# Loads of the sums in another order, stores of the down-projection on GpSimd's queue, and one pause more in the last norms, in a one-core decoder layer

## The chip, the cores and the metric

One Trainium2 chip; the kernel uses one of its cores. The metric is the device time of one execution in microseconds, as the median of several runs. The engines are called PE (TensorE's matmuls, with PEld for its weight loads), DVE (VectorE), ACT (ScalarE), POOL (GpSimd) and SP (the queue that issues nearly all DMAs).

## What is computed

A decoder layer over x of 1 x 2048 x 1024 in float32: two token mixers side by side, an output projection, a feed-forward part with a short causal convolution, and a final norm.

```python
def _conv_ffn(h, w_up, conv_w, conv_b, w_down):
    u = h @ w_up                                   # 1024 -> 2 x 2816
    u = causal_depthwise_conv(u, conv_w) + conv_b  # width 3
    gate, val = jnp.split(u, 2, axis=-1)
    return (jax.nn.silu(gate) * val) @ w_down      # 2816 -> 1024

def reference(x, ...):
    proj = _rmsnorm(x, norm1_w) @ w_in
    o_hg = _hgrn2_mixer(...)     # gated linear recurrence
    o_rw = _rwkv7_mixer(...)     # data-dependent decay, delta rule
    x = x + jnp.concatenate([o_hg, o_rw], axis=-1) @ w_out
    x = x + _conv_ffn(_rmsnorm(x, norm2_w), w_up, conv_w, conv_b, w_down)
    return _rmsnorm(x, final_norm_w)
```

## The kernel before

**Stages.** The 2048 tokens are four blocks of 512 (`b` = 0 to 3). Phase 1 (to some 1380 us) computes the mixers; the output projection of the last block follows (to some 1444 us), then the up-projection with convolution and gate (to some 2325 us), then the down-projection and the final norm (to the end). Every float32 matrix product is made of three matmuls (lines 262 to 264, `mm3`): an operand is split into a high part by ScalarE (line 246) and a low part by VectorE (line 247), and high x high, high x low and low x high are added up.

**The up-projection** (`run`, line 1345 on) has 44 iterations n: two halves of the tokens (two blocks each) x 22 groups of 128 columns. Each multiplies 2 x 2 blocks by a scheme of seven products instead of eight. A product (`prod`) is 4 x 3 = 12 matmuls of 128 x 512, so an iteration is 84 matmuls; the accumulators are called ua, ub and ud. Of each iteration's last two products and of its convolution (`late`: line 1424 on, the `y` of lines 1441 and 1442) the program speaks after the next iteration's first product. The result of the gate goes to DRAM as `gd` (line 1449).

**Side work.** After each product `aside(n)` (line 1305) takes one item off a list; an empty item is a pause of one product. Items are taken from n = 1 on, and none at n = 20 to 22. The list holds, in this order:
- `norm_last`, four times (blocks 2 and 3, two halves each): load two tiles `xt2` of x, pause, scale one tile, scale the other (line 1253), pause, then eight pairs of transposes on PE (`tp`, line 256), each with an eviction and a store to `h2d`. 13 items each.
- `four`, 15 times: load four tiles, pause, two items of VectorE work and four stores, pause: 5 items. They make the second half's transformed activations `Ts` and the transformed down weights `Tw`.
- `sums(g, kk)`, from n = 23 on: of the gate's results of one token half g the four tiles a11, a12, a21, a22 (first index the block, second the half of the 2816 columns) are loaded from `gd`, combined by four VectorE operations (line 1293), and each result is stored to `Sg` right after its operation (line 1294). 7 items: the loads, two pauses, four operations. Group 0 has all its kk = 0 to 10 there (n = 23 to 33), group 1 has kk = 0 to 6, one for each of n = 36 to 42.

All these tiles come from the ring `br`, six buffers of 128 x 512 that are given out in the order of release (`raw_`, line 1121). So a list of loads also says which tile gets a free buffer first. A tile scheduler sets the order on each engine. SP works through its queue in order: a DMA that waits holds all behind it.

**The down-projection** (line 1453 on) takes steps 5 to 142. A step needs one tile of gate results or sums and one of weights (`draw`, line 1462, six buffers per name), split into `da` and `db`, for 12 matmuls; `load(s_ + 4)` and `take(s_ + 2)` run ahead. The last four `sums` of group 1 are made here by `g_sums` (four `sraw` loads, four operations at lines 196 to 199, four stores at line 201), at four steps six apart. When the last product of a tile of tokens is done, `finish` scales the finished rows (line 1491) and stores them, 512 KB each (line 1493): eight stores for the first half of the tokens, in mid-stage, eight for the second, at the end. The residual tiles `xt3` (line 1476) have twelve buffers for sixteen tiles, so the last four loads go into buffers that the first half's output was stored from.

Of the kernel before, what the change touches and what calls it, by code (L numbers as in the profile page):

```python
# [18 lines left out]
P = 128  # L19
T = 2048  # L20
D = 1024
KD = D // P
# [39 lines left out]
def tile_layer(ctx, tc, consts, x, norm1_w, w_in, hg_lb_logits, hg_norm_w, rw_shift_mu, rw_w0, rw_w2,  # L62
               rw_a0, rw_a2, rw_g2, rw_k_k, rw_k_a, rw_r_k, rw_ln_w, rw_ln_b, w_out, norm2_w, w_up,
               conv_w, conv_b, w_down, final_norm_w, out, pairs=(0, 1, 2, 3), heads=(0, 1, 2, 3),
               stages=("1", "2"), dbg=None):
    nc = tc.nc
    V, S, TE = nc.vector, nc.scalar, nc.tensor
    dma = nc.sync.dma_start

    cp = ctx.enter_context(tc.tile_pool(name="cp", bufs=1, reuse_waits="tile"))  # L70
    dp = ctx.enter_context(tc.tile_pool(name="dp", bufs=1, space=DRAM))
# [22 lines left out]
    def pst(name):  # L94
        return pools["ps"].tile([P, 512], F32, tag="mm", name=name, bufs=8)
# [13 lines left out]
    def act(out_, in_, func, **kw):  # L109

        want = tables.get(func)
        if want is not None and want != tab["now"]:
            pre = S.preload_act_table_set(want)
            for u_ in tab["uses"]:
                tc.add_manual_dep(pre.ins, u_.ins.name, NOSYNC, reason="table order")
            tab.update(now=want, pre=pre, uses=[])
        i_ = S.activation(out_, in_, func, **kw)  # L117
        if want is not None:
            tc.add_manual_dep(i_.ins, tab["pre"].ins.name, NOSYNC, reason="table order")
            tab["uses"].append(i_)  # L120
        return i_

    def rstd(pool, xt, name, sqt="nsq", sqb=1):

        sq = pool.tile([P, D], BF16, tag=sqt, name="nsq", bufs=sqb)
        st = pool.tile([P, 2], F32, tag="nst", name=name, bufs=8)
        act(sq, xt, AF.Square, accum_out=st[:, 0:1])
        act(st[:, 1:2], st[:, 0:1], AF.Ln, bias=eps6, scale=1.0 / D)
        act(st[:, 1:2], st[:, 1:2], AF.Exp, scale=-0.5)
        return st[:, 1:2]  # L130
# [48 lines left out]
    gd_ = [dp.tile([FF, BLK], F32, name=f"gd{b}") for b in range(NBLK)]  # L179
# [3 lines left out]
    Sg = [[dp.tile([KH * P, BLK], F32, name=f"Sg{g}{i}") for i in range(4)] for g in range(2)]  # L183
    Tw = [dp.tile([KH * P, BLK], F32, name=f"Tw{i}") for i in range(4)]

    def krows(t_, q, kk):

        return t_[(q * KH + kk) * P:(q * KH + kk + 1) * P, :]
# [4 lines left out]
    def g_sums(tile_, g, kk):  # L193

        a11, a12, a21, a22 = (tile_(krows(gd_[2 * g + u], q, kk)) for u in range(2) for q in range(2))
        V.tensor_add(a22, a21, a22)
        V.tensor_sub(a21, a11, a21)
        V.tensor_sub(a11, a22, a11)
        V.tensor_sub(a12, a12, a11)
        for i, t_ in enumerate((a22, a11, a21, a12)):  # L200
            dma(krows(Sg[g][i], 0, kk), t_)


    DP = (("a", (0, 0), (0, 0)), ("b", (0, 1), (1, 0)), ("a", 1, 1), ("b", 0, 0), ("a", 2, 2), ("a", (1, 1), 3),
# [904 lines left out]
    with ExitStack() as c2:  # L1109
# [11 lines left out]
        def raw_(src):  # L1121
            t_ = hr.tile([P, BLK], F32, tag="br", name="br", bufs=6)
            if src is not None:
                loader[0](t_, src)
            return t_
# [20 lines left out]
        with tc.tile_pool(name="op", bufs=1, reuse_waits="tile") as op_:  # L1146
# [52 lines left out]
            for dh in range(2):  # L1199
                accs = [pst("wacc") for _ in range(4)]  # L1200
                for n, k in enumerate((0, 1, 4, 5, 2, 3, 6, 7)):
# [3 lines left out]
                    if n == 5:  # L1205
                        for i in range(4):
                            t0 = b * BLK + i * P
# [11 lines left out]
                    if dh == 1 and 2 <= n:  # L1219
                        for j in range(2):  # L1220
                            q = 2 * (n - 2) + j
# [9 lines left out]
        with tc.tile_pool(name="up", bufs=1, reuse_waits="tile") as up:  # L1231
# [7 lines left out]
            def aside_of(fs):  # L1239

                side.extend((first_at[0], f) for f in fs)

            def norm_last(b, i2):

                xt = []

                def load():
                    for q in range(2):
                        xt.append(up.tile([P, D], F32, tag="xt2", name="xt2", bufs=2))
                        dma(xt[q], x1d[b][(i2 * 2 + q) * P:(i2 * 2 + q + 1) * P, :])  # L1250

                def scale(q):
                    V.tensor_scalar_mul(xt[q], xt[q], rstd(hr, xt[q], "nst", "br", 6))

                def evict(k, tp, w):
                    t_ = hr.tile([P, 256], F32, tag="br", name="h2", bufs=6)
                    act(t_, tp, AF.Copy, scale=w)
                    dma(h2d[b][k * P:(k + 1) * P, i2 * 256:i2 * 256 + 256], t_)

                g = transposed(xt, "n2", lambda: pst("tp"), evict)  # L1260
                aside_of([load, None, lambda: scale(0), lambda: scale(1), None] + [lambda: next(g)] * KD)

            def four(srcs, make, dsts):

# [13 lines left out]
            QB = [(q, b) for q in range(2) for b in range(2)]  # L1278
# [8 lines left out]
            def sums(g, kk):  # L1287

                ts = []
                ops = ((3, V.tensor_add, 2, 3), (2, V.tensor_sub, 0, 2), (0, V.tensor_sub, 3, 0), (1, V.tensor_sub, 1, 0))  # L1290

                def op(d, f, a, b, i):
                    f(ts[d], ts[a], ts[b])
                    dma(krows(Sg[g][i], 0, kk), ts[d])

                aside_of([lambda: ts.extend(raw_(krows(gd_[2 * g + u], q, kk)) for u, q in QB), None, None]
                         + [lambda o=o, i=i: op(*o, i) for i, o in zip((0, 2, 1, 3), ops)])

            for g in range(2):
# [155 lines left out]
    with tc.tile_pool(name="dn", bufs=1, reuse_waits="tile") as dn:  # L1455
        ops, xts, pend, m2 = {}, {}, [], {}
# [32 lines left out]
        def finish(g, u, i):  # L1489
            t_ = xts.pop((g, u, i))  # L1490
            V.scalar_tensor_tensor(t_, t_, rstd(dn, t_, "fst"), fw, ALU.mult, ALU.mult)
            t0 = (2 * g + u) * BLK + i * P
            dma(out[0, t0:t0 + P, :], t_)

        def evict(g, p, accs, i):

# [20 lines left out]
        for s_ in range(DS, N):  # L1517
            g, p, kk = steps[s_]
# [60 lines left out]
```

## Time and profile before

| | |
|---|---|
| median of 3 runs | 2740.66 us (2735.97 to 2741.07) |
| the profiled execution | 2734.05 us; its span 2732.2 us |
| granted TensorE clock, mean | 0.991 |
| busy: PE, DVE, ACT, POOL | 96%, 69%, 49%, 13% of the span |
| DMA | 517.88 MB, mean 190 GB/s |

The profile is of one execution, which was 6.6 us shorter than the median of the runs; 1.85 us of it lie around the span. In a row of waits an engine's idle time is put down to what came last before it went on: `PE ua L262 <- ACT m L117: 5.6, 6, 1.5` says that PE, about to run line 262 into `ua`, waited for the ScalarE instruction that wrote `m`, for 5.6 us in total, 6 times, 1.5 us at the longest. A timeline row has start, duration, engine, line, operation and, in brackets, the idle time before it.

### The profile page before, as it was taken

How to read it: one execution, taken by the hardware profiler on the slowest of the kernel's cores; microseconds unless marked ns; L12 is line 12 of the kernel's file. 1: busy time of each engine (PE TensorE's matmuls, PEld its weight loads, DVE VectorE, ACT ScalarE, POOL GpSimd, SP SyncE). 2: the span in 40 equal slices, each digit the busy share in tenths (PEclk: the TensorE clock that was granted, in tenths of full speed). 3: DMA queues.
4: the chain of work that ended last, by engine and by line, in shares of the span. 5: the costliest groups of instructions: out<-in, count | busy, mean ns of one | idle time of the engine just before them, and what ended most of it. 6: DMA issues, size and time to landing. Idle time of an engine off the chain costs nothing.

```text
span 2732.2 us, 47983 instructions
## 1 busy us (share of the span) xinstructions
PE 2631.2 (96%) x18059; PEld 2097.0 (77%) x18059; DVE 1896.6 (69%) x3665; ACT 1348.1 (49%) x2168; POOL 367.5 (13%) x660
## 2 busy tenths in 40 slices
PE   7989999989999999999899999999999999999998
PEld 5767777767777767777677788887888877788887
DVE  4856656566456654756668789988888888677556
ACT  4546443444544335334456765456555445445444
POOL 6433222212321113222100000000000000000000
PEclk9999999999999999999999999999999999999999
DMA  8655544354663546854576358746655454898665
GB/s 299 198 162 165 171 138 134 115 147 156 215 199 105 138 140 212 280 143 132 165 245 192 119 193 268 234 151 222 222 187 194 132 191 131 287 320 289 213 193 185
DMA packets 365438, 517.88 MB, mean 190 GB/s; under 512 B 97439, under 2 KB 194069, under 8 KB 365205
## 3 DMA queue, kind: packets, MB, share of 16 engines
q1 hardware_dynamic: 313265, 345.39, 39.4%
q0 software_dynamic: 51872, 169.41, 19.2%
q8 instruction: 142, 2.33, 0.4%
q14 instruction: 91, 0.75, 0.1%
q10 hardware_dynamic: 68, 0.02, 0.0%
HBM read 376.27 MB, written 138.41 MB: 188 GB/s over the span
## 4 chain that ended last, share of the span: by engine, by line
PE 68%; DVE 11%; DMA 9%; issue 6%; ACT 4%; SPq 1%; POOL 1%; DVEq 0%; ACTq 0%; POOLq 0%
PE pj L262 8%; PE pj L263 7%; PE pj L264 7%; PE ua L262 4%; PE ua L264 4%; PE ua L263 4%; PE da L262 3%; PE da L263 3%; PE da L264 3%; PE ud L264 2%; PE ud L262 2%; PE ud L263 2%; PE db L263 2%; PE db L262 2%; PE db L264 2%
## 5 line engine op out<-in xcount | busy, mean ns | idle before, releaser
L262 PE MATMUL pj<-hh,wh 128*128 128x512 f32 x960 | 402.7, 420 | 2.2 <-ACT rkv L117 1.1
L263 PE MATMUL pj<-hl,wh 128*128 128x512 f32 x960 | 378.4, 394 | 0.0
L264 PE MATMUL pj<-hh,wl 128*128 128x512 f32 x960 | 378.4, 394 | 0.0
L262 PE MATMUL ua<-Bh,uwh 128*128 128x512 f32 x704 | 276.7, 393 | 7.2 <-ACT m L117 5.6
L264 PE MATMUL ua<-Bh,uwl 128*128 128x512 f32 x704 | 274.4, 390 | 0.0
L263 PE MATMUL ua<-Bl,uwh 128*128 128x512 f32 x704 | 274.2, 389 | 0.0
L262 PEld LDWEIGHTS pj<-hh,wh 128*128 128x128 f32 x960 | 181.0, 189 | 55.6 <-issue 12.2
L264 PEld LDWEIGHTS pj<-hh,wl 128*128 128x128 f32 x960 | 181.0, 189 | 40.1 <-DMA wl<-Win170l 0.6
L263 PEld LDWEIGHTS pj<-hl,wh 128*128 128x128 f32 x960 | 181.4, 189 | 39.1 <-issue 6.2
L246 ACT CAST uwh<-uraw 128x512 fp32r<-128x512 f32 x220 | 134.5, 617 | 139.3 <-PE ua L263 61.8
L247 DVE TENSOR_TENSOR dal<-draw,dah 128x512 fp32r<-128x512 f32 x138 | 95.3, 690 | 112.5 <-ACT dah L246 112.3
L247 DVE TENSOR_TENSOR uwl<-uraw,uwh 128x512 fp32r<-128x512 f32 x220 | 147.1, 686 | 36.3 <-ACT uwh L246 36.3
L246 ACT CAST dah<-draw 128x512 fp32r<-128x512 f32 x138 | 85.8, 622 | 166.2 <-PE da L263 74.5
L262 PEld LDWEIGHTS ua<-Bh,uwh 128*128 128x128 f32 x704 | 132.2, 188 | 37.4 <-ACT m L117 8.9
L264 PEld LDWEIGHTS ua<-Bh,uwl 128*128 128x128 f32 x704 | 132.1, 188 | 28.2 <-DVE uwl L247 0.4
L263 PEld LDWEIGHTS ua<-Bl,uwh 128*128 128x128 f32 x704 | 132.3, 188 | 26.7
L262 PE MATMUL ud<-Bh,uwh 128*128 128x512 f32 x352 | 137.7, 391 | 0.0
L264 PE MATMUL ud<-Bh,uwl 128*128 128x512 f32 x352 | 137.1, 389 | 0.0
L263 PE MATMUL ud<-Bl,uwh 128*128 128x512 f32 x352 | 137.0, 389 | 0.0
L263 PE MATMUL da<-dbl,dah 128*128 128x512 f32 x332 | 129.5, 390 | 0.2 <-DVE dbl L247 0.2
L264 PE MATMUL da<-dbh,dal 128*128 128x512 f32 x332 | 129.2, 389 | 0.0
L1449 POOL DMA_DIRECT2D gd<-y x2 | 1.1, 554 | 952.0 <-DVE y L1447 952.0
(567 smaller groups left out, 6189.3 us busy)
## 6 DMA issues: line engine op xcount, KB each, us to landing
uraw<-in_w_up_dram SPq DMA_DIRECT2D x176, 256.0 KB, 3.3
woraw<-in_w_out_dram POOLq DMA_DIRECT2D x96, 256.0 KB, 3.5
br<-gd SPq DMA_DIRECT2D x88, 256.0 KB, 4.4
draw<-Sg SPq DMA_DIRECT2D x88, 256.0 KB, 3.3
draw<-Tw SPq DMA_DIRECT2D x88, 256.0 KB, 3.4
gd<-y SPq DMA_DIRECT2D x86, 256.0 KB, 2.9
Sg<-br SPq DMA_DIRECT2D x72, 256.0 KB, 2.3
xt<-x1d SPq DMA_DIRECT2D x32, 512.0 KB, 6.5
```

Of the source, the lines that this page charges most:

```text
L246: S.copy(hi, src)
L247: V.tensor_sub(lo, src, hi.bitcast(F32))
L262: TE.matmul(acc, lh, rh, start=first, stop=False, skip_group_check=skip)
L263: TE.matmul(acc, lh, rl, start=False, stop=False, skip_group_check=skip)
L264: TE.matmul(acc, ll, rh, start=False, stop=last, skip_group_check=skip)
L1449: (dma if end is None else nc.gpsimd.dma_start)(gd_[2 * h + b][fb * P:(fb + 1) * P, :], ys[0][:, b * BLK:(b + 1) * BLK])
```

## The change

```diff
-    dma = nc.sync.dma_start
+    dma, store = nc.sync.dma_start, nc.gpsimd.dma_start
...
         for i, t_ in enumerate((a22, a11, a21, a12)):
-            dma(krows(Sg[g][i], 0, kk), t_)
+            store(krows(Sg[g][i], 0, kk), t_)
...
-                aside_of([load, None, lambda: scale(0), lambda: scale(1), None] + [lambda: next(g)] * KD)
+                aside_of([load, None, lambda: scale(0), lambda: scale(1), None, None] + [lambda: next(g)] * KD)
...
-                ops = ((3, V.tensor_add, 2, 3), (2, V.tensor_sub, 0, 2), (0, V.tensor_sub, 3, 0), (1, V.tensor_sub, 1, 0))
+                ops = ((1, V.tensor_add, 0, 1), (0, V.tensor_sub, 2, 0), (2, V.tensor_sub, 1, 2), (3, V.tensor_sub, 3, 2))
...
-                aside_of([lambda: ts.extend(raw_(krows(gd_[2 * g + u], q, kk)) for u, q in QB), None, None]
+                aside_of([lambda: ts.extend(raw_(krows(gd_[2 * g + u], q, kk)) for u, q in QB[2:] + QB[:2]), None, None]
...
-            dma(out[0, t0:t0 + P, :], t_)
+            (dma if g else store)(out[0, t0:t0 + P, :], t_)
```

Four parts. The norms get one pause more before their transposes, so each has 14 items, two whole iterations. The sums load a21, a22, a11, a12 instead of a11, a12, a21, a22; `ops` is renumbered for it, and the four operations are the same ones in the same order (a22 = a21 + a22, a21 = a11 - a21, a11 = a22 - a11, a12 = a12 - a11). The stores of `g_sums` (16 of 256 KB) and the first half's output stores (8 of 512 KB) are issued by GpSimd instead of SP.

**The sums of group 1, SP.** One iteration between n = 36 and 42; `gd_156` holds a11 and a12, `gd_157` a21 and a22, and `Sg_162` to `Sg_165` are where the four results go. Before:

```order
L1141 DMA uraw<-in_w_up_dram 128x4x128
L1124 DMA br<-gd_156 128x512
L1124 DMA br<-gd_157 128x512 x2
L1294 DMA Sg_165<-br 128x512
L1124 DMA br<-gd_156 128x512
L1294 DMA Sg_162<-br 128x512
L1294 DMA Sg_164<-br 128x512
L1141 DMA uraw<-in_w_up_dram 128x4x128
L1294 DMA Sg_163<-br 128x512
```

Now:

```order
L1141 DMA uraw<-in_w_up_dram 128x4x128
L1124 DMA br<-gd_157 128x512
L1124 DMA br<-gd_156 128x512 x2
L1124 DMA br<-gd_157 128x512
L1294 DMA Sg_162<-br 128x512
L1294 DMA Sg_164<-br 128x512
L1294 DMA Sg_163<-br 128x512
L1294 DMA Sg_165<-br 128x512
L1141 DMA uraw<-in_w_up_dram 128x4x128 x3
```

Before, a group of loads was a12, a21 and a22, and the next kk's a11 came behind a store of the kk before; now it is a22, a11 and a12, with the next kk's a21 right behind, and the four stores stand together.

**The same iteration, VectorE.** Line 1293 is an operation of the sums, `uwl` the low part of an up weight, `y1` the convolution's first accumulation. In the numbered names of the rows before, br_22574 is a11, 22576 a12, 22578 a21 and 22580 a22:

```order
L247 TENSOR_TENSOR uwl_22435<-s1_22412,uwh_22434 128x512
L1293 TENSOR_TENSOR br_22580<-br_22578,br_22580 128x512
L1293 TENSOR_TENSOR br_22578<-br_22574,br_22578 128x512
L247 TENSOR_TENSOR uwl_22452<-uraw_22306,uwh_22451 128x512
L1293 TENSOR_TENSOR br_22574<-br_22580,br_22574 128x512
L1441 SCALAR_TENSOR_TENSOR y1_22375<-cv_22213,cvt_14639,y1_22375 128x1024
```

In the rows now, br_22572 is a21, 22574 a22, 22576 a11 and 22578 a12:

```order
L247 TENSOR_TENSOR uwl_22433<-s1_22410,uwh_22432 128x512
L1293 TENSOR_TENSOR br_22574<-br_22572,br_22574 128x512
L1293 TENSOR_TENSOR br_22572<-br_22576,br_22572 128x512
L1293 TENSOR_TENSOR br_22576<-br_22574,br_22576 128x512
L1293 TENSOR_TENSOR br_22578<-br_22578,br_22576 128x512
L247 TENSOR_TENSOR uwl_22450<-uraw_22304,uwh_22449 128x512
L1441 SCALAR_TENSOR_TENSOR y1_22373<-cv_22211,cvt_14639,y1_22373 128x1024
```

The third operation moves ahead of the weight split, and the fourth, which before ran in the next iteration (ahead of that iteration's `uwl` of `s1`), joins the block.

**The first `g_sums` in the down-projection, SP.** `draw` are a step's two loads, `sraw` the loads of the sums, `xt` a residual tile. The piece of the difference, with - for rows of before and + for rows of now (the tile `xt` only has another number):

```order
-L1477 DMA xt_23623<-x1d_147 128x1024
-L201 DMA Sg_162<-sraw 128x512
-L201 DMA Sg_163<-sraw 128x512
-L201 DMA Sg_164<-sraw 128x512
-L201 DMA Sg_165<-sraw 128x512
+L1477 DMA xt_23621<-x1d_147 128x1024
 L1462 DMA draw<-Sg_159 128x512
 L1462 DMA draw<-Tw_167 128x512
```

The four stores stood between two steps' loads; now the next step's loads follow the residual tile directly. The same four rows stand on GpSimd's queue, where nothing else is left by then.

**The third norm, PE.** `tp` are the transposes of one 128 x 128 piece, `ua` and `ud` accumulators. The first transposes before:

```order
L262 MATMUL ud<-Bh_14661,uwh 128x512
L263 MATMUL ud<-Bl_14662,uwh 128x512
L264 MATMUL ud<-Bh_14661,uwl 128x512
L256 MATMUL tp<-ident,xt_16037 128x128
L262 MATMUL ua<-Bh_14664,uwh 128x512
L263 MATMUL ua<-Bl_14665,uwh 128x512
```

And now:

```order
L262 MATMUL ua<-Bh_14658,uwh 128x512
L263 MATMUL ua<-Bl_14663,uwh 128x512
L264 MATMUL ua<-Bh_14658,uwl 128x512
L256 MATMUL tp<-ident,xt_16072 128x128
L256 MATMUL tp<-ident,xt_16074 128x128
L262 MATMUL ud<-Bh_15084,uwh 128x512
```

They stood between an iteration's sixth and seventh product and now stand behind the second product of the next round, three products on: one for its own pause and one for each of the two norms ahead of it. Its loads move two products on, so from load to transposes it is one product more.

## The prediction

> **What bounds the kernel now.** I read the busy table first, then the stages as windows, then what TensorE waited for.
>
> ```profile
> PE 2631.2 (96%) x18059; PEld 2097.0 (77%) x18059; DVE 1896.6 (69%) x3665; ACT 1348.1 (49%) x2168; POOL 367.5 (13%) x660
> ```
>
> ```profile
> 1600.00:1800.00 200.00, 199.94 (x887) 165.15 (x886) 188.97 (x299) 104.12 (x152) 0.00 (x0) 1.00 0.75 246
> 1988.41:2140.73 152.32, 152.32 (x673) 126.13 (x672) 134.37 (x197) 77.53 (x112) 0.00 (x0) 1.00 0.53 171
> 2140.73:2283.15 142.42, 138.13 (x604) 112.72 (x603) 119.04 (x175) 67.66 (x100) 0.00 (x0) 1.00 0.56 183
> ```
>
> The window rows give length, then busy time of PE, PEld, DVE, ACT and POOL, clock, DMA share and GB/s. I set their bounds on the VectorE addition of line 1408, which runs once in every iteration n of the up-projection. The second is eight iterations with the sums of group 0: 152.32 / 8 = 19.04 us each, and PE is busy for all of it. The third is seven iterations (from n = 35's addition to n = 42's) with the sums of group 1: 142.42 / 7 = 20.35 us each, PE idle for 4.29 us, the clock full in both. So TensorE sets the pace nearly everywhere, and the change can win only where TensorE waits. Those places from the up-projection on:
>
> ```profile
> PE ua L262 <- ACT m L117: 5.6, 6, 1.5
> PE fa L263 <- DVE uwl L247: 2.6, 2, 1.6
> PE da L262 <- ACT dbh L246: 2.4, 1, 2.4
> PE ua L262 <- ACT uwh L246: 1.5, 1, 1.5
> PE tp L256 <- DVE xt L1253: 1.0, 1, 1.0
> ```
>
> Columns: total, times, longest. The six waits of 5.6 us are all in the sums of group 1 (the window 2140.73 to 2302 alone gives the same row); the 2.4 stands at 2384 in the down-projection; the 1.0 is the third norm's. These three, 9.0 us together, are what the edits touch. The `fa` waits (at n = 22) and the `ua` wait for `uwh` (at the first iteration) stay: no edit moves anything there. In phase 1, before 1380 us, nothing changes.
>
> **Part 1, the pause (line 1261).** Each of four norms gets one empty slot more between its scaling and its transposes. A slot is one product, 12 matmuls. This is the chain around the third norm's first transposes (start, duration):
>
> ```profile
> 1555.57 0.76 DVE xt L1253
> 1556.34 0.04 issue
> 1556.38 0.55 PE tp L256 x3
> 1556.93 0.23 PE ua L262
> ```
>
> The scaling (`xt`) ends at 1556.33 and the transposes start at 1556.38, after 0.96 us of idle TensorE (the row of 1.0 above). One product is 12 x 0.23 = 2.8 us. Put behind another product, the transposes would be due 1.8 us after the scaling is done: the wait goes, **-0.96**. Nothing else is late there, for the matmuls that move ahead have their operands (the same iteration has no other wait). The other three norms did not wait before and get more room. The bounds are 0 (if VectorE comes to the scaling as much later) and -0.96; I take -0.96, as with 14 slots, two whole iterations, every norm stands in the phase of the first one, which did not wait.
>
> The queue of side work grows by four slots: 4 x 14 + 15 x 5 = 131 slots, and n = 1 to 19 have 19 x 7 = 133. So the transformed tiles (`four`) run four products later and still end in n = 19. I cost that at nothing: their loads and stores are SP's and TensorE is busy 199.94 of 200 us there. The cover is VectorE's remaining 11 us in 200, about 1 us per iteration; if the new phase were worse, the nearest row is a wait like the norm's, 1.0 us, up to three times: 0 to +3, I take 0.
>
> **Part 2, the order of the sums' loads (lines 1290 and 1296).** In the sums of group 1 VectorE, not TensorE, sets the 20.35 us:
>
> ```profile
> DVE br L1293 <- DMA br<-gd: 22.0, 7, 3.7
> ```
>
> ```profile
> 2170.01 0.69 DVE L247 TENSOR_TENSOR uwl<-s,uwh 128x512 fp32r<-128x512 f32 x1
> 2174.07 1.42 DVE L1293 TENSOR_TENSOR br<-br 128x512 f32<-128x512 f32 x2 [3.38 <-DMA br<-gd]
> 2175.41 0.68 DVE L247 TENSOR_TENSOR uwl<-uraw,uwh 128x512 fp32r<-128x512 f32 x1
> 2176.01 0.68 DVE L1293 TENSOR_TENSOR br<-br 128x512 f32<-128x512 f32 x1
> 2176.61 1.28 DVE L1441 SCALAR_TENSOR_TENSOR y<-cv,cvt,y 128x1024 f32<-128x1024 f32 x1
> ```
>
> ```profile
> 2168.05 1.41 SPq L1124 DMA_DIRECT2D br<-gd  x3
> 2169.98 0.32 SPq L1294 DMA_DIRECT2D Sg<-br  x1
> 2170.35 0.42 SPq L1124 DMA_DIRECT2D br<-gd  x1
> ```
>
> VectorE works 119.04 / 7 = 17.0 us per iteration and waits 3.4 for `br`; 17.0 + 3.4 = 20.4. The first of a tile's four operations (2174.07) adds a21 to a22. SP issues a12, a21 and a22 from 2168.05 in 1.41 us, 0.47 each: a22 is the **third**, asked for at 2169.0, there at 2174.0; behind a store follows the next k's a11 (2170.35). In the new program a21 is loaded an iteration ahead and a22 is the first of the group, then a11 and a12; the four operations stand in one block.
>
> With the same issue times a22 is asked for at 2168.05 and a11 and a12 at 2168.5 and 2169.0. The first load of a group shares the engines with fewer. Its ends: the 5.0 us of the third (landing at 2173.0), and the 3.3 of SP's weight loads of this size (the `uraw` row below; landing at 2171.4). The operations take 0.69 each, a12 is needed by the fourth alone and lands at 2174.0 as the third load did. With the early end three operations run before 2174.0, the fourth ends at 2174.7, `uwl` runs, and `y` starts at 2175.3 instead of 2176.61: 1.3 saved. With the late end four operations end at 2175.8 and `y` starts at 2176.4: 0.2 saved. I take **0.8** per iteration, about the middle. VectorE's cycle becomes 20.35 - 0.8 = 19.55 us (19.05 to 20.15) against TensorE's 19.04.
>
> Before, VectorE fell behind by 7 x (20.35 - 19.04) = 9.2 us, and TensorE lost 5.6: so 3.6 us were covered by products whose operands were ready. Now it falls behind by 7 x 0.51 = 3.6 us, just that cover; I leave 0.3 for an uneven iteration: **-5.3**. At 20.15 the lag would be 7.8, of which 4.2 are lost, so the bounds are -1.4 and -5.6.
>
> In the sums of group 0 no wait reached TensorE (152.32 of 152.32 busy). The new program asks for all tiles of the next k there an iteration ahead, so I cost it at nothing; what hides a wait there is VectorE's idle time, (152.32 - 134.37) / 8 = 2.2 us per iteration. What it costs if this cover goes is the third rival.
>
> **Part 3, the stores of the late sums (line 201).** SP around the first of four, its wait, and TensorE behind it:
>
> ```profile
> 2374.57 0.32 SPq L1477 DMA_DIRECT2D xt<-x1d  x1
> 2378.75 2.98 SPq L201 DMA_DIRECT2D Sg<-sraw  x4
> 2381.84 0.39 SPq L1462 DMA_DIRECT2D draw<-Sg  x1
> 2382.33 0.40 SPq L1462 DMA_DIRECT2D draw<-Tw  x1
> ```
>
> ```profile
> SPq L201 <- DVE sraw L196: 3.5, 1, 3.5
> ```
>
> ```profile
> 2386.66 1.20 PE L262 MATMUL da<-dbh,dah 128*128 128x512 f32 x4 [2.44 <-ACT dbh L246]
> ```
>
> SP is free at 2374.89, but its next instruction is a store that waits for the sums, until 2378.75. The loads for the step behind it are issued at 2381.84 and 2382.33, and TensorE, idle for 2.44, starts at 2386.66. Without the stores SP can go on from 2374.89, or when a tile of the ring is free, up to 6.9 us before 2381.84; 2.44 of them are enough: **-2.44**. What is late next are the draws of the step after it, 3 us on for TensorE but issued 0.5 us on by SP, so they hold. The bounds are -2.44 and 0 (if the ring of six, not the stores, held the draws). The other three groups have no wait of TensorE behind them.
>
> The Trainium skill (DMA: Bandwidth & Descriptors, section "Issuing engines are not separate DMA queues") speaks against this: issuing from another engine saves only the sequencer's time for the issue. By it the gain would be four issues, 4 x 0.32 = 1.3 us. The rows differ: SP stands still from 2374.89 to 2378.75, for a wait and not for an issue.
>
> **Part 4, the stores of the output's first half (line 1493),** with what is known of GpSimd's stores:
>
> ```profile
> L1449 POOL DMA_DIRECT2D gd<-y x2 | 1.1, 554 | 952.0 <-DVE y L1447 952.0
> woraw<-in_w_out_dram POOLq DMA_DIRECT2D x96, 256.0 KB, 3.5
> uraw<-in_w_up_dram SPq DMA_DIRECT2D x176, 256.0 KB, 3.3
> SPq L1493 <- DVE xt L1491: 10.7, 8, 1.6
> 2400.00:2500.00 100.00, 100.00 (x441) 82.10 (x440) 68.44 (x103) 50.90 (x92) 0.00 (x0) 1.00 0.86 295
> ```
>
> SP waited 10.7 us for these eight stores, and TensorE lost nothing (the last row, and no wait after 2400): 0. On GpSimd 24 issues cost 24 x 0.554 = 13.3 us, of an engine with nothing else to do. New is that SP's later loads into these tiles wait for the landing of another queue's store, 3.5 us by the `woraw` row against at most 1.6 per store that SP waits today: between 0 and +1.9, hidden by the same lead, so 0. The last stores stay on SP, so the tail stays.
>
> **Sum:** -0.96 - 5.3 - 2.44 = -8.7 us, from the profiled execution's 2734.05 (its span 2732.2 and 1.85 around it) to 2725.4. The median of before is 6.6 above that execution: 2740.66 - 8.7 = **2732.0**.
>
> **The rivals.**
> First, VectorE stays as slow in group 1: the fourth operation waits as long as the first did, for a12 is now third in the group. For it speaks that the landing of the third load is unchanged, against it that three operations run under the wait. Then only 0.96 and 2.44 are won: 2737.3 (2735.9 with the 1.4 of the lower bound).
> Second, SP finds another wait in the down-projection (the ring of six, or a landing of GpSimd's stores) and part 3 brings nothing: 6.3 won, 2734.4. For it speaks that SP waits for `dal` and `dbl`, the ring's readers, elsewhere; against it that 2.44 of 6.9 us are enough. The Trainium skill (SBUF — State Buffer, section "SBUF: two separate sides") holds that a DMA from GpSimd's queue starves while VectorE's two-port mode locks GpSimd out, which would lead here; the `woraw` and `uraw` rows, 3.5 and 3.3, show little of it.
> Third, on the other side: in the sums of group 0 the four stores now stand together on SP, ahead of the next loads. If VectorE waits there 3.4 us per iteration as it does in group 1, this is 1.2 more than its idle 2.2 in each of 11 iterations, 13 us, less the cover of 3.6: +9.6. The same wait would leave group 1 as it was, so +9.6 - 3.4 = +6.2: 2746.9. It decides from 2.5 us of waiting per iteration on. Against it: those loads are asked for an iteration, 19 us, ahead.
>
> **How the numbers follow.** A difference under 0.2%, 5.5 us, can't be told from none. The forecast has 0.55, the first rival 0.18, the second 0.12, the third 0.15. Faster by over 0.2%: 0.52 of the forecast, half of the second and 0.03 of partial gains in the first, 0.61. Slower: the third, 0.15. Same: 0.24. The range: below, the sum of the best ends (-9.0) and the 6.6 by which the profiled execution lay under the median, 2725; above, between the first rival (2737.3) with a phase loss of 3 and the third's price, 2743.
>
> **What would show it.** Part 1: no `tp` wait for `xt`. Part 2: iterations 35 to 41 at 19.0 to 19.5 us and the `br` wait under 2.6 us each; wrong if the `ua` waits for `m` stay. Part 3: no `da` wait for `dbh` at 2384. The prediction fails if iterations 26 to 34 take longer than 19.04 us, or 9 to 19 show new waits.

## The result, and the profile after

The changed kernel takes **2728.34 us** (median of 10 runs, 2718.84 to 2732.08) against 2737.25 us (median of 10, 2731.65 to 2751.1; the three runs shown ahead of the prediction are among them). The ratio is **0.9948, 95% interval 0.9932 to 0.9964**: faster by 0.36 to 0.68%, or 10 to 19 us. The two medians alone differ by 8.9 us, 0.33%, just below that interval; the ratio is used below, and where the choice matters the text says so. A second set of runs of the same program gave 0.9941 (0.9927 to 0.9956). The prediction was 2732.0 with a range of 2725 to 2743 and a gain of 8.7 us (0.32%): the time fell into the range, the direction was right, and by the ratio the gain was too small. The profiled execution took 2722.71 us, its span 2720.9.

The busy table of the page, and what TensorE waited for from 1390 us on (total, times, longest):

```profile
PE 2632.7 (97%) x18059; PEld 2101.4 (77%) x18059; DVE 1897.4 (70%) x3665; ACT 1344.9 (49%) x2166; POOL 380.8 (14%) x684
```

```profile
PE fa L263 <- DVE uwl L247: 2.6, 2, 1.6
PE ua L262 <- ACT m L117: 1.8, 4, 0.6
PE wacc L264 <- DVE Bl L240: 1.3, 1, 1.3
PE fa L262 <- ACT uwh L246: 1.2, 1, 1.2
PE wacc L263 <- DVE wol L240: 1.1, 1, 1.1
PE ua L262 <- ACT uwh L246: 0.5, 1, 0.5
PE da L263 <- DVE dbl L247: 0.2, 1, 0.2
```

The `tp` wait for `xt` (1.0) and the `da` wait for `dbh` (2.4) are gone, and the `ua` waits for `m` fell from 5.6 to 1.8, of which 1.2 lie in the sums of group 1; the other 0.6 is a single wait at 1475 us (n = 2), which before did not have. POOL has 24 instructions and 13.3 us more (660 and 367.5 before), as worked out. Two windows, again cut at line 1408: from n = 27's addition to n = 34's, with the last sums of group 0, and from there to n = 41's. (These are the numbers when the 44 additions are counted from n = 0; the prediction calls the same additions one higher, n = 35 and n = 42.)

```profile
2004.43:2137.71 133.28, 133.28 (x589) 110.38 (x588) 115.04 (x167) 67.80 (x98) 0.00 (x0) 1.00 0.46 152
2137.71:2275.10 137.39, 136.54 (x600) 112.07 (x599) 121.14 (x177) 68.18 (x100) 0.00 (x0) 1.00 0.58 192
```

133.28 / 7 = 19.04, so group 0 did not slow down (the third rival is out). 137.39 / 7 = 19.63 against 20.35 before and 19.55 predicted. VectorE's wait in the second window, and one iteration of it on VectorE:

```profile
DVE br L1293 <- DMA br<-gd: 14.0, 7, 2.9
```

```profile
2168.74 2.87 DVE L1293 TENSOR_TENSOR br<-br 128x512 f32<-128x512 f32 x4 [1.53 <-DMA br<-gd]
2171.53 0.68 DVE L247 TENSOR_TENSOR uwl<-uraw,uwh 128x512 fp32r<-128x512 f32 x1
2172.13 1.28 DVE L1441 SCALAR_TENSOR_TENSOR y<-cv,cvt,y 128x1024 f32<-128x1024 f32 x1
```

The four operations run as one block, without a wait inside, and the wait ahead of them is 2.0 us per iteration instead of 3.1 (14.0 / 7 and 22.0 / 7). The chain of work just ahead of that block (start, duration) shows something that the prediction had not seen:

```profile
2160.67 1.16 DVE y L1447
2161.83 0.02 issue
2161.84 0.34 SPq L1449
2162.18 0.05 issue
2162.23 2.93 DMA gd<-y
2165.16 0.02 issue
2165.18 3.47 DMA br<-gd
```

The loads of the sums start the moment the gate's store (line 1449) has landed, 2165.18 after 2165.16. In the down-projection SP now goes straight on behind the residual tile, while GpSimd's queue waits for VectorE in its place:

```profile
2366.63 0.32 SPq L1477 DMA_DIRECT2D xt<-x1d  x1
2367.31 0.32 SPq L1462 DMA_DIRECT2D draw<-Sg  x1
2368.01 0.32 SPq L1462 DMA_DIRECT2D draw<-Tw  x1
2368.68 0.32 SPq L1462 DMA_DIRECT2D draw<-Sg  x1
2369.36 0.32 SPq L1462 DMA_DIRECT2D draw<-Tw  x1
```

```profile
2371.05 0.54 POOL L201 DMA_DIRECT2D Sg<-sraw  x1 [34.47 <-DVE sraw L196]
2371.78 0.54 POOL L201 DMA_DIRECT2D Sg<-sraw  x1 [0.18 <-issue]
```

Two steps' loads are out before the first store's data exists (2371.05). One later load of a residual tile waits 1.2 us for a landing of GpSimd's output stores; TensorE does not notice.

### The profile page after: what moved, and what is told of

Read it like the earlier page. It is cut to its first block, busy times and chain, and to the rows that moved or that the text cites. A ratio compares the mean times of both kernels' runs of the same rounds, so it can differ in the third digit from the quotient of the medians.

```text
span 2720.9 us, 48003 instructions
## 1 busy us (share of the span) xinstructions
PE 2632.7 (97%) x18059; PEld 2101.4 (77%) x18059; DVE 1897.4 (70%) x3665; ACT 1344.9 (49%) x2166; POOL 380.8 (14%) x684
## 4 chain that ended last, share of the span: by engine, by line
PE 73%; DMA 8%; DVE 7%; issue 5%; ACT 4%; POOL 1%; SPq 1%; DVEq 0%; POOLq 0%; ACTq 0%
PE pj L262 8%; PE pj L263 7%; PE pj L264 7%; PE ua L264 4%; PE ua L262 4%; PE ua L263 4%; PE da L262 3%; PE da L263 3%; PE da L264 3%; PE ud L262 2%; PE ud L263 2%; PE ud L264 2%; PE db L264 2%; PE db L263 2%; PE db L262 2%
## 5 line engine op out<-in xcount | busy, mean ns | idle before, releaser
L262 PEld LDWEIGHTS pj<-hh,wh 128*128 128x128 f32 x960 | 182.3, 190 | 55.1 <-issue 13.3
```

What stands on the lines that cost most here:

```text
L262: TE.matmul(acc, lh, rh, start=first, stop=False, skip_group_check=skip)
```

## The experiments

Each experiment is one profile and, but for the last, five rounds of runs beside the kernel before. This table holds TensorE's waits of each profile, read from the same four windows: `tp` for `xt` at the third norm (1480 to 1590 us), `ua` for `m` in the transformed tiles (1600 to 1800), `ua` for `m` in the sums of group 1 (2130 to 2315), `da` for `dbh` in the down-projection (2330 to 2690). Two columns of lengths stand beside them, in us. "Eight n" goes from n = 34's addition at line 1408 to n = 42's: eight iterations that hold all sums of group 1, 152.32 us if each takes 19.04. "Stage" is the down-projection from its first matmul (`da<-uwh`) to the end of its last.

| kernel | norm | tiles | sums 1 | down | eight n | stage | ratio to before (95%) |
|---|---|---|---|---|---|---|---|
| before | 1.0 | 0 | 5.6 | 2.4 | 159.8 | 398.8 | |
| before again (e6) | 0.9 | 0 | 6.9 | 2.3 | 161.4 | 399.3 | 1.0000 (0.9986 to 1.0015) |
| pause only (e1) | 0 | 0.3 | 6.7 | 2.9 | 161.1 | 401.0 | 0.9982 (0.9968 to 0.9997) |
| shift only (e5) | 1.0 | 0 | 6.4 | 2.7 | 160.6 | 400.1 | 0.9987 (0.9975 to 0.9999) |
| order only (e2) | 1.1 | 2.0 | 0.5 | 2.3 | 153.9 | 400.0 | 0.9968 (0.9955 to 0.9980) |
| late sums' stores only (e3) | 1.0 | 1.2 | 6.1 | 0 | 160.8 | 396.2 | 0.9982 (0.9965 to 0.9999) |
| late sums' stores later on SP (e8) | 0.7 | 2.8 | 6.3 | 0 | 160.5 | 395.6 | 0.9962 (0.9945 to 0.9979) |
| output stores only (e4) | 0.8 | 1.5 | 5.9 | 2.4 | 160.1 | 399.9 | 0.9991 (0.9975 to 1.0008) |
| a22 second (e9) | 1.0 | 1.3 | 3.8 | 2.8 | 158.6 | 398.9 | 0.9997 (0.9980 to 1.0013) |
| old order, loads on GpSimd's queue (e11) | 1.1 | 0.7 | 11.5 | 2.0 | 166.9 | 398.9 | 1.0023 (1.0007 to 1.0039) |
| old order, sums held (e14) | 1.0 | 0.7 | 0 | 2.6 | 152.3 | 400.3 | 0.9963 (0.9947 to 0.9979) |
| old order, other rows (e15) | 1.0 | 0 | 0 | 2.1 | 152.3 | 398.6 | one run |
| changed | 0 | 0 | 1.2 | 0 | 154.8 | 395.6 | 0.9948 (0.9932 to 0.9964) |
| changed again (e7) | 0 | 0 | 0.8 | 0 | 154.0 | 395.5 | 0.9941 (0.9927 to 0.9956) |
| changed, output stores on SP (e12) | 0 | 0.2 | 0 | 0 | 153.4 | 396.0 | 0.9958 (0.9941 to 0.9976) |
| changed, loads on GpSimd's queue (e10) | 0 | 0.3 | 2.1 | 0 | 155.5 | 397.0 | 0.9957 (0.9940 to 0.9973) |
| changed, sums held (e13) | 0 | 0 | 0 | 0 | 152.3 | 395.5 | 0.9949 (0.9932 to 0.9966) |

The ratios are coarse beside these terms (e8 and e3 lose the same wait and differ by 0.002, with intervals that overlap), so the verdicts below rest on the waits and the lengths first. In e10 TensorE also waited 0.9 us for `dbl` in the down-projection, which no column shows.

### The four parts, one by one

**e1, the pause alone.**

```diff
-                aside_of([load, None, lambda: scale(0), lambda: scale(1), None] + [lambda: next(g)] * KD)
+                aside_of([load, None, lambda: scale(0), lambda: scale(1), None, None] + [lambda: next(g)] * KD)
```

> Only the pause is added. Theory: the third norm's transposes no longer wait (before 0.96 us for the scaling), all other waits stay as before, so the up-projection is 1.0 us shorter and the rest equal; the median moves by -1.0 us, too little to be told from none. Also looked at: TensorE's new wait of 0.6 us at n = 2 in the changed kernel; if the pause brings it, it stands here too, if it is chance it does not. Rival (the four later slots cost something in the transformed tiles, n = 9 to 19): new waits of 1 us or more there and no gain.

Measured: no wait at the norms, 0.3 in the transformed tiles, no wait at n = 2 (the 0.6 of the changed kernel stands again in e7, 0.7, and not in e10, e12 and e13, which have the pause too, so it comes and goes), a ratio of 0.9982. The gain at the norm is the one predicted. The ratio is a gain of 0.8 to 8.8 us, which 1.0 us fits only at its edge.

**e2, the order alone** (the two lines of `sums` of the diff above).

> Only the sums' loads take the new order. Theory: the waits for m in the sums of group 1 fall from 5.6 us to about 1.2 as in the changed kernel, VectorE's waits for br from 22.0 to about 14, and the stretch from n = 35 to n = 43 gets 4.4 to 4.9 us shorter; the gap at the third norm (0.96) and the one in the down-projection (2.44) stay. Median -4.5 us. Rival (the gain there comes from other parts too, for instance from four slots of phase): the waits fall by less than 3 us.

```profile
DVE br L1293 <- DMA br<-gd: 12.9, 7, 2.3
```

Measured: VectorE's wait 12.9, TensorE's 0.5, the other two gaps where they were, 1.1 and 2.3. The eight iterations are 5.9 us shorter than in the first profile of before, where 4.4 to 4.9 had been expected. The order alone does it.

**e3, the stores of the late sums alone** (the line of `g_sums`).

> Only the stores of the late sums go by GpSimd's queue. Theory (SP stood still behind stores that waited for VectorE): the gap of 2.44 us in the down-projection goes, and with the small ones behind it 3.1 us of TensorE's time from the first step to the last matmul (398.8 us before, 395.6 in the changed kernel); nothing else moves; median -3 us. Rival (only the time of the issues is saved, 4 x 0.32): 1.3 us there, and a gap of 1.1 us stays.

Down-projection, 2380 to 2430 us, before and in e3 (length, PE, PEld, DVE, ACT, POOL, clock, DMA):

```profile
2380.00:2430.00 50.00, 47.56 (x209) 38.60 (x208) 32.27 (x51) 21.13 (x34) 0.00 (x0) 1.00 0.91 313
```

```profile
2380.00:2430.00 50.00, 49.78 (x220) 40.89 (x219) 36.97 (x59) 24.65 (x40) 7.58 (x14) 1.00 0.97 344
```

Measured: the gap is gone, 220 matmuls instead of 209 in the same 50 us, 11 x 0.227 = 2.5 us. The whole stage took 396.2 us instead of 398.8 and 399.3 in the two profiles of before (expected was 395.6). The 1.1 us that the rival would leave are not there.

**e4, the output's stores alone.**

> Only the first half's output stores go by GpSimd's queue. Theory: no change anywhere, 0 +- 0.3 us in the down-projection (398.8 us from its first to its last matmul), the gap of 2.44 stays. Rival (SP's 10.7 us of waiting for them did cost, in small restarts of TensorE after 2400, or the later loads of residual tiles now wait): a change of 0.5 us or more there, either way.

Measured: all gaps as before and a ratio that holds 1. The stage took 399.9 us, 0.6 and 1.1 more than in the two profiles of before. That is over the 0.5 that the expectation gave the rival, but the ten kernels with the old stores of the late sums lie between 398.6 and 401.0, so one profile can't resolve it. No wait shows a cost or a gain of these stores in either queue; an effect under 1 us is not excluded. e12, further down, asks the same from the other side.

### The pause's second effect

The runs without the pause had lost 1.2 to 2.0 us in the transformed tiles, where the first profile of before showed none. Two kernels ask whether this is the phase.

**e5**, the norms as before, four empty slots behind them:

```diff
+            aside_of([None] * 4)
             for kk in range(4):
                 four([hsrc(1, q, b, kk) for q, b in QB], t_make, t_out(lambda i, kk=kk: tdst(1, i, kk)))
```

> The kernel before with four empty slots between the norms and the transformed tiles, and no pause in the norms: the transformed tiles stand where the change puts them, the norms where they were. In the runs with one part of the change each, the three without the pause lost 1.4 to 2.3 us of TensorE at 1677 to 1745 us, in the transformed tiles, which the first profile of the kernel before does not show; the one with the pause lost 0.4 there. Theory (the pause's second effect is this shift): no loss over 0.5 us between 1600 and 1800, the third norm's gap of 1.0 stays; median -1.5 to -2.5 us. Rival (it is chance from run to run, not the phase): a loss of 1.3 us or more there in this run too, or none in the other run of the kernel before.

**e6**, the kernel before again:

> The kernel before unchanged, for a second profile. Theory (phase): TensorE loses 1.3 to 2.3 us between 1660 and 1760, as in the three runs with its phase, and the first profile was the lucky one. Rival (chance): any value from 0 up. The other places as in the first profile: 1.0 at the third norm, 5 to 8 in the sums of group 1, 2.4 to 3.1 in the down-projection. Ratio 1.000 within 0.0015.

Measured: no wait there in e5, and none in e6 either. So a single profile cannot tell. In all ten kernels with the old phase the instructions of each engine stand in the same order up to 1900 us. Over all of them: the ten profiles with the old phase lost 0, 0, 2.0, 1.2, 2.8, 1.5, 1.3, 0.7, 0.7 and 0, a mean of 1.0 us; the seven with the phase of the change 0.3, 0, 0, 0, 0.2, 0.3 and 0, a mean of 0.1. The old phase waits in some executions and not in others, the new one hardly in any: 0.9 us on the mean. Both theories held a part: chance decides whether there is a wait, and with the new phase it is rare. That the phase does this by giving VectorE more room is our reading; no run measured the room. Nor do the two profiles of the kernel before itself show a loss to win back, 0 and 0: the 0.9 stands on its variants.

**e7**, the changed kernel again:

> The changed kernel unchanged, for a second profile and a second ratio. By the terms of the single parts (pause 1.0 to 1.4 at the norms and 1.5 to 2 in the transformed tiles, order 4.5 to 5.2, late sums' stores 2.6 to 3.1, output stores 0) the sum is 10 to 12 us, ratio 0.9956 to 0.9964. Rival (the 8.7 of the prediction is the whole): 0.9968.

Measured: 0.9941, a little more than the sum of the single waits (below).

### A wait, or the time of the issues?

**e8** keeps the late sums' stores on SP, three steps later:

```diff
-            dma(krows(Sg[g][i], 0, kk), t_)
+            held.append((krows(Sg[g][i], 0, kk), t_))
...
+            if s_ - 3 in sums_at:
+                for d_, t_ in held:
+                    dma(d_, t_)
+                held.clear()
             if s_ in sums_at:
                 g_sums(d_raw("sraw"), 1, sums_at[s_])
```

> The kernel before with the late sums' four stores still on SP, but issued three steps later, behind the loads of the next steps: as many issues by SP as before, and no wait of SP for VectorE in front of a step's loads. Theory (the wait, not the issues, made the gap): the gap of 2.4 us goes and the down-projection takes about 396 us, as with GpSimd's queue. Rival (an issuing engine of its own saves only the time of the issues): the down-projection stays at 398.8 to 400, since no issue is saved.

Measured: as many issues on SP as before, and the gap is gone all the same. The stage took 395.6 us, as expected, and the 50 us from 2380 hold 222 matmuls instead of 209. It was the wait in front of the loads, not the time of four issues. The Trainium skill's sentence on issuing engines (DMA: Bandwidth & Descriptors, "Issuing engines are not separate DMA queues") does not cover a queue in which a store's wait holds up the loads behind it.

### What sets the wait of the sums of group 1

The prediction's step was the place of a22 in SP's group of loads. **e9** puts it second: the loads in the order a21, a11, a12, a22 give the groups a12, a22, next a21, next a11.

> The kernel before with the sums' loads in the order a21, a11, a12, a22: SP's group in an iteration is then a12, a22, and the next kk's a21 and a11; a22 is the second of the group instead of the third (before) or the first (changed). Theory (where a22 stands in the group sets VectorE's wait): VectorE's wait for br lies between 22.0 (before) and 14.0 (changed), about 17 to 19 us over the seven iterations, and TensorE loses 3 to 5 us there instead of 7 to 9 or 2. Rival (what helps is the block of four operations and four stores, which stand nearly as in the changed kernel): the wait is about 14 as there.

```profile
DVE br L1293 <- DMA br<-gd: 12.9, 5, 3.2
DVE br L1293 <- issue: 6.3, 2, 4.1
```

Measured: 12.9 + 6.3 = 19.2 us (the second row is two waits whose end the profile doesn't name), TensorE 3.8, between third (22.0 in the first profile of before; TensorE 5.6 to 6.9) and first (12.1 to 14.0; 0 to 1.2). The place counts, as expected, though 19.2 is just above the 17 to 19 given.

**e10** and **e11** take the loads of group 1 off SP, in the new and in the old order:

```diff
+                def fetch():
+                    loader[0] = store if g else dma
+                    ts.extend(raw_(krows(gd_[2 * g + u], q, kk)) for u, q in QB[2:] + QB[:2])
+                    loader[0] = dma
```

> The changed kernel with the loads of group 1's sums on GpSimd's queue. On SP they stand behind a weight load that waits for VectorE (line 1417); on GpSimd's queue they wait for free tiles alone. Theory (it is the time of issue, set by SP's order, that makes VectorE wait): the wait for br falls from 14 us to under 2, the iterations take 19.04 us, and TensorE loses under 0.5 us in the sums of group 1 instead of 1.6 to 2.4; median 1.5 to 2 us under the changed kernel. Rival (the loads are slow because the DMA engines are busy then): the wait stays over 8.

> The kernel before, with its order of loads, and only the loads of group 1's sums on GpSimd's queue. Theory: the order no longer matters, VectorE's wait for br is under 2 us and TensorE loses under 0.5 there, more won than by the new order (7 to 8 us instead of 5 to 6). Rival (the order matters by itself): the wait stays above 14.

VectorE's waits in e10, then in e11, and what GpSimd's queue waited for in e10:

```profile
DVE br L1293 <- issue: 12.3, 5, 3.9
DVE br L1293 <- DMA br<-gd: 3.5, 2, 2.1
```

```profile
DVE br L1293 <- DMA br<-gd: 19.8, 5, 5.7
DVE br L1293 <- issue: 7.5, 2, 3.9
```

```profile
POOL br L1124 <- DMA gd<-y: 121.8, 4, 69.6
POOL br L1124 <- issue: 51.9, 3, 17.7
```

Both expectations failed: 15.8 and 27.3 us, no less than on SP (the rows that end in `issue` are waits whose end the profile doesn't name). The last fence says why. Nothing stands ahead of these loads on GpSimd's queue, and still they wait, four times of seven for `gd<-y`, the store of the gate. The row of a tile in the second half of the columns (a12 and a22) is written in the same iteration in which the sums are run, so in these two kernels SP's order is not what holds the loads. On GpSimd's queue the first load starts half a microsecond behind the landing (2168.76, then 2169.32), and the four follow 0.53 apart, here in e10 from the chain and from the queue:

```profile
2165.47 3.29 DMA gd<-y
...
2169.32 0.51 POOL br L1124
```

```profile
2169.32 2.12 POOL L1124 DMA_DIRECT2D br<-gd  x4 [17.90 <-DMA gd<-y]
```

So a load late in its group lands later still, and e11, with a22 as third, got worse: 11.5 us of TensorE.

Three kernels then tested that the rows are the cause. **e13** and **e14** hold each operation of group 1's sums behind the gate multiplication spoken last, in the changed kernel and in the one before; **e15** lets the old kernel read rows that were stored long ago, so its result is not that of the layer:

```diff
-                    f(ts[d], ts[a], ts[b])
+                    i_ = f(ts[d], ts[a], ts[b])
+                    if g:
+                        tc.add_manual_dep(i_.ins, gate[0].ins.name, NOSYNC, reason="late sums")
...
-                        V.tensor_mul(ys[0], ys[0], ys[1])
+                        gate[0] = V.tensor_mul(ys[0], ys[0], ys[1])
```

```diff
-                aside_of([lambda: ts.extend(raw_(krows(gd_[2 * g + u], q, kk)) for u, q in QB), None, None]
+                aside_of([lambda: ts.extend(raw_(krows(gd_[u], q, kk)) for u, q in QB), None, None]
```

> The changed kernel in which each operation of group 1's sums is held, in VectorE's order, behind the multiplication of the gate (line 1447) that was spoken before it, so it stands later than now. In the traces each group of loads starts within 0.1 us of the landing of the gate's store (line 1449) whose rows it reads, in either queue and either order. Theory (the sums run as soon as the rows are there, and VectorE pays store and load, 2.9 and 3.4 us, in every iteration): with the operations later, the wait for br falls from 13 us to under 2, TensorE loses under 0.5 us there instead of 1.5 to 2.4, ratio 0.0005 to 0.0008 under the changed kernel's. Rival (SP's order and the ring set the wait): it stays above 8 us.

> The same hold in the kernel before, with its order of loads and nothing else of the change. Theory: the order of loads matters only while a load is waited for, so here too the wait for br is under 2 us and TensorE's loss in the sums of group 1 falls from 7 to 9 us to under 0.5; the two gaps at the third norm and in the down-projection stay. Ratio 0.997. Rival (the order is worth something by itself): more than 1.5 us of loss stays there.

> The kernel before, but the sums of group 1 read the rows of the first token half, which have long been stored, so their results are those of other rows; number, size and order of the loads and operations are as before. Theory (the wait is for the rows): VectorE's wait for br goes from 22 us to under 2 and the iterations take 19.04 us. Rival (a22 is third in its group, whatever the rows): the wait stays near 22.

All that VectorE waited for between 2137 and 2300 us in e13, in e14 and in e15:

```profile
DVE uwl L247 <- ACT uwh L246: 13.6, 11, 2.0
DVE y L1443 <- ACT y L117: 9.8, 9, 1.1
```

```profile
DVE uwl L247 <- ACT uwh L246: 12.4, 11, 2.0
DVE y L1443 <- ACT y L117: 8.7, 8, 1.1
```

```profile
DVE uwl L247 <- ACT uwh L246: 13.4, 12, 2.0
DVE y L1441 <- ACT y L117: 9.7, 9, 1.1
```

Measured: no wait for `br` in any of the three, and none of TensorE in the sums of group 1, in the old order as in the new. The eight iterations take 152.3 us in all three, not a tenth more than TensorE needs. In e13 and e14 the operations start 18.9 us behind the issue of the gate's store, instead of 8.9 in the kernel before and 6.9 in the changed one (2185.23 after 2166.29 in e13, 2174.07 after 2165.17, 2168.74 after 2161.84), so store and loads have long landed. What VectorE paid for was the time from the store to the end of the load, and a later use pays none of it. e15 shows less than was expected of it. Without the dependence the scheduler also set another order: the loads of one group are issued from 2162.80 to 2165.60 and the operations start at 2178.06, so the order of loads and operations is not "as before", and e15 alone doesn't tell the rows from the place. That the landing of the store releases the loads is shown by the waits of GpSimd's queue in e10 and by SP's own in the changed kernel (next section). The expectation of e13 also had every group start within 0.1 us of the landing; that holds in the changed kernel (2165.18 after 2165.16), while GpSimd's queue started 0.55 later, and in the kernel before a22's load started 0.7 later. e13 has the fewest waits of all kernels in the four windows; its ratio, 0.9949 (0.9932 to 0.9966), cannot be told from the changed kernel's.

**e12**, the changed kernel with the output stores back on SP:

```diff
-            (dma if g else store)(out[0, t0:t0 + P, :], t_)
+            dma(out[0, t0:t0 + P, :], t_)
```

> The changed kernel with the first half's output stores back on SP. Theory (these stores cost nothing in either queue): the down-projection takes 395.6 us as in the changed kernel and the ratio is the changed kernel's, 0.994 to 0.995. Rival (they are part of the gain beyond the single terms): the down-projection takes 0.5 us longer or the ratio is 0.001 or more higher.

Measured: no wait of TensorE in the down-projection beyond the 0.2 us that the changed kernel has too, and a stage of 396.0 us, 0.4 and 0.5 more than in the changed kernel's two profiles, at the edge of what the rival asked. The ratio, 0.9958, is higher by 0.0010 and 0.0017 than the changed kernel's two, with intervals that overlap. By the waits the stores cost nothing; half a microsecond can't be told from none here.

## Why the prediction was right or wrong

**Right:** where TensorE would win. Of the three places named, two gaps vanished, and the third shrank from 5.6 to 1.2 us; the output's stores, the tail and the sums of group 0 did not move, and none of the three rivals came.

**The step that failed is the price of a wait.** The prediction took each place to be worth the idle time in TensorE's rows ("TensorE lost 5.6: so 3.6 us were covered"; "2.44 of them are enough: -2.44"). The lengths of the stages say that more was lost there. The eight iterations with the sums of group 1, then the down-projection, each before and then in the changed kernel:

```profile
2140.73:2300.54 159.81, 154.16 (x673) 125.68 (x672) 134.31 (x197) 76.10 (x112) 0.00 (x0) 1.00 0.55 180
2137.71:2292.49 154.78, 153.56 (x673) 125.85 (x672) 135.81 (x197) 76.62 (x112) 0.00 (x0) 1.00 0.56 186
```

```profile
2325.90:2724.70 398.80, 396.12 (x1741) 325.76 (x1740) 251.45 (x376) 193.23 (x349) 1.10 (x2) 1.00 0.75 249
2317.90:2713.50 395.60, 395.32 (x1741) 326.16 (x1739) 250.45 (x377) 192.79 (x349) 14.03 (x26) 1.00 0.75 251
```

Without a wait eight iterations take 152.32 us. Before took 159.81: TensorE lost 7.5 us where its rows show 5.6, for the same 673 matmuls were also busy for 154.16 us instead of 152.32. So of the 9.2 us by which VectorE fell behind, 1.7 were covered and not 3.6. In the changed kernel VectorE fell behind by 137.39 - 133.28 = 4.1 us (3.6 predicted) and TensorE lost 154.78 - 152.32 = 2.5 (0.3 predicted): the cover is 1.6 again.

**Part 2** is then worth more than its row. The seven profiles with the old order of loads on SP took 159.8 to 161.4 us for the eight iterations, 160.6 on the mean, the four with the new one 153.4 to 154.8, 154.0 on the mean: **-6.5** instead of -5.3, outside the bounds of -1.4 to -5.6 (in TensorE's rows alone, 6.3 and 0.6, it is about -5.6).

**Part 3** had the right cause and the same fault in size. The row of 2.44 was read rightly: ten profiles with the old stores waited 2.0 to 2.9 us for `dbh`, and none with the stores off the path did. But the stage took 398.6 to 401.0 us in those ten, 399.6 on the mean, and 395.5 to 397.0 in the seven others, 395.9 on the mean: **-3.7**, where -2.44 was given as the most. A part of the difference is at the gap itself: the last matmul ahead of it started at 2383.83 and the next one at 2386.66, where 0.23 is the usual distance, which is 2.60 lost for a wait of 2.44.

```profile
2383.83 0.40 PE L264 MATMUL da<-dbh,dal 128*128 128x512 f32 x1
2386.66 1.20 PE L262 MATMUL da<-dbh,dah 128*128 128x512 f32 x4 [2.44 <-ACT dbh L246]
```

The rest comes in steps of 0.1 to 0.5 us up to 2445, by the matmul starts of both profiles of before against both of the changed kernel. What stretches these matmuls was not tested.

**The mechanism of part 2** was half right. The step "SP's order and the place of a22" predicted 0.8 us less wait per iteration; it was 1.1 (22.0 - 14.0 over 7). The place counts (e2, e9). In the profile of before it was also what held a22:

```profile
2165.17 0.81 SPq L1449 DMA_DIRECT2D gd<-y  x2
2167.58 0.38 SPq L1141 DMA_DIRECT2D uraw<-in_w_up_dram  x1
```

The second of the two stores, with a22's row, was issued at 2165.56 and landed 2.8 us later, at 2168.4; SP came to a22's load at 2169.08. What the prediction did not see is that a22 in first place would be held by that landing instead. SP's waits for it in front of these loads, before and in the changed kernel:

```profile
SPq L1124 <- DMA gd<-y: 0.5, 1, 0.5
```

```profile
SPq L1124 <- DMA gd<-y: 3.8, 7, 0.8
```

So a22 was asked for 2.95 us behind the issue of its store (2165.18 after 2162.23) instead of 3.52, 0.6 earlier and not the 1.0 predicted. Its load made up for that: 3.47 us to its landing as the first of four, against 4.88 as the third of three.

**Part 1** was mis-sized too. The prediction costed the four later slots of the transformed tiles at "0 to +3, I take 0", because TensorE was busy 199.94 of 200 us there. The mean of ten profiles is a loss of 1.0 us and the new phase leaves 0.1, so the term is **-0.9** on the mean, outside the bounds given for it; up to -2.8 in a single execution, and 0 in both profiles of the kernel before. The norm itself was right: 1.0 us, gone.

**The sum** of the measured means, the first two from TensorE's rows and the other two from the lengths, is -1.0 - 0.9 - 6.5 - 3.7 = -12.1 us, 0.44%, against the 8.7 predicted. That lies in the interval of the first set of runs (0.36 to 0.68%) and at the lower end of that of the second (0.44 to 0.73%).

**What stays open** is the rest, some 2 to 4 us by the two ratios (by the medians of the first set there is none). The two profiles of before and the two of the changed kernel have spans of 2737.5 and 2722.5 us on the mean, 15.0 apart. Of this 4.7 lie in phase 1, 6.7 between the output projection and the down-projection and 3.5 in the down-projection. Phase 1 is the largest source of scatter: each engine's instructions stand there in the same order in all these programs, and yet the first matmul of the output projection started at 1397.1 us in e9 and at 1382.8 in e15.

```profile
L262 PE MATMUL wacc<-woh,Bh x64: 388/390/629, 1397.1 to 1444.8; 128*128 128x512 f32 x64
```

```profile
L262 PE MATMUL wacc<-woh,Bh x64: 388/389/478, 1382.8 to 1429.2; 128*128 128x512 f32 x64
```

(The first and last start stand behind the durations.) A difference of 14 us that no edit made is as large as the whole change. Over all profiles phase 1 took 1389.6 us on the mean with the whole change (five) and 1390.5 without (twelve), so the 4.7 may well be chance; that phase 1 gains something was not shown.

**The baseline.** The forecast was set on 2740.66, the median of three runs; the ten of the result gave 2737.25, and four later sets of 17 to 35 runs 2739.4 to 2740.5. The time predicted, 2732.0, is 3.7 us above the 2728.34 measured. Against the ten runs, 3.4 of that is the baseline and 8.7 us would be nearly the whole difference of the medians; against the later sets the baseline is about right, and it is the gain that is too small. That the time fell into the range is in part luck and says little about the terms.

## What to carry to other kernels

A queue that is served in order should hold no store whose data isn't there yet ahead of a load that is needed soon: put the store later, or on an idle queue; both removed the same gap. When an engine waits for a load, follow the chain back past the load: if it starts at the landing of a store, its place in a queue is worth a part (here 6.5 of the 8.3 us lost), and a later use of it is worth all. The idle time in a row of waits was less than the waits cost here; the length of the stage against the same stage without them gives the whole. One or two profiles in which a nearly full stage lost nothing don't show that it loses nothing: here seven of ten lost something.

## What had not been expected of the hardware

The same instructions of phase 1 took 1382.8 to 1397.1 us in the profiles, 1% of its length, in executions with a mean granted clock of 0.986 to 0.993. Loads issued by GpSimd's queue started 0.55 us behind the landing they waited for (e10) and 0.53 apart, SP's 0.02 (changed kernel) and 0.4 to 0.5; yet 24 stores on GpSimd's queue, off every path, cost nothing that the waits show. A wait of 2.44 us in TensorE's row went with a stage 3.2 us longer, and waits of 5.6 us with 7.5 us lost.
